# A hybrid HGRN2 / mLSTM / mixture-of-experts block: VectorE takes GpSimd's elementwise work, a head's sums use two PSUM rings, and three output tiles are added by DMA

## The chip, the cores and the metric

The kernel runs on one core of a Trainium2 chip. A core has a matrix engine (TensorE; PE in the rows, PEld for its weight loads), VectorE (DVE), ScalarE (ACT), GpSimd (POOL) and a queue engine (SyncE, SP) that issues most DMAs. Each engine runs its own instructions strictly in order, and engines wait for each other through semaphores. The metric is device microseconds (us) of one execution, lower is better; the time of a kernel is the median of its runs.

## The reference

The block works on 1024 tokens (16 more "meta" tokens stand in front) of width 1024, in fp32. Cut to what matters:

```python
h = layer_norm(concat([meta, x]))
proj = h @ w_in                                   # one wide projection, split in twelve
f = lb + (1 - lb) * sigmoid(f_a)                  # forget gate, 8 heads of 128
o_a = hgrn2(q_a, 1 - f, i_a, log(f))              # linear recurrence, decay per key channel
y_a = head_norm(o_a) * silu(g_a)                  # g_a is the projection GA in the kernel
h_b = mlstm(conv(q_b), conv(k_b), v_b, gates)     # 4 heads
y_b = head_norm(h_b) * sigmoid(o_b)               # o_b is the projection OB
mix = (sigmoid(gate_a) * (y_a @ w_a) + sigmoid(gate_b) * (y_b @ w_b)) @ w_out
h = layer_norm(ALPHA * h + mix)                   # first layer norm (ln1)
ffn = routed_experts(h) + shared_expert(h)        # 64 experts, 8 for each token
out = layer_norm(ALPHA * h + ffn)                 # last layer norm (ln2): gain g, bias b
```

## The kernel before

Every matrix product is made of three products of fp32r parts: a weight tile is split by ScalarE into a high part `wh` (a rounding copy) and by a subtraction into a low part `wl = raw - wh`. `load_slab` brings one 1024x512 slab of a weight as four pieces of 128x1024 through `split_weights` (lines 185 to 198): DMA on SP, `wh` on ACT (line 195), `wl` on VectorE or, for the pieces named by `SLAB_POOL = (1, 3)`, on GpSimd (line 196). There are 28 such slabs. The shared expert's six pieces do the same with `SHARED_POOL`, which adds three, so GpSimd makes 59 of these 118 subtractions.

The work runs in this order. (1) Embedding: layer norm of token tiles, transposes, first projection; GpSimd adds the bias there, and this is not touched. (2) The GA projection; `gate_out` (line 412) computes `silu(pm) * row` from the PSUM tile `pm`: sigmoid on ACT, a copy of `pm` on ACT, two products on GpSimd (lines 423, 424). Beside it `mlstm_gates` (line 507) computes the mLSTM gates with a few small matmuls (lines 530, 531), a chain on ACT and VectorE, and transposes (line 559). (3) Twice: projections F and Q, then four heads of `hgrn_head`. A head builds its score matrix `st` in seven doubling levels `lv` (lines 711 to 757). At each level VectorE makes `qp` (line 725), GpSimd makes `ks` (line 727), PE multiplies both into a PSUM tile (line 739), VectorE copies the result under a mask into `st` (line 742), GpSimd updates the suffix product (line 756) and VectorE the prefix product (line 757). The next level needs both. At the end of a head (lines 786 to 799) the output is made in two halves: PE sums `st`·`v` and `q`·`sts` into a PSUM tile from `ps_o`, a ring of one buffer, ACT takes sums of squares, VectorE a reciprocal root in 13 small steps (lines 116 to 127), and then `g = po * root * g` (line 799) frees the tile. (4) The remaining projections (the OB one with `gate_out` too), convolution, four mLSTM heads, gates. (5) The two branch products, the output product, ln1 (`layer_norm`, line 157, whose addition is on GpSimd for tiles 5, 6, 7), routing, the shared expert. (6) The routed experts, whose order on PE, GpSimd and SP is written out by hand. GpSimd there issues gathers (line 1359) and scatters that add into DRAM (line 1438). (7) The last layer norm, whose order on VectorE, ACT and GpSimd follows the table `TAIL`.

Outside the stretches whose order is written out, a scheduler sets the order of each engine's instructions when the program is built, from its own costs of the instructions. So a changed instruction also moves its neighbours.

In the last layer norm the eight token tiles `zf` are loaded by eight DMAs in turn. In `TAIL`, ('A', i) takes tile i's statistics on ACT (three instructions, `ACT_STATS`), ('S', i) takes them on VectorE, a group such as (('C2','C3','S4'), (0,1,2,3)) centres tiles on VectorE and between them runs the root of four tiles, and ('F', i) finishes a tile:

```python
if i in ADD_DVE:    # 3, 5, 7
    nc.vector.scalar_tensor_tensor(zs[i], zs[i], factor[i], b_ln2, op0=OP.mult, op1=OP.add)
else:
    nc.scalar.activation(zs[i], zs[i], AF.Copy, scale=factor[i])
    nc.gpsimd.tensor_add(zs[i], zs[i], b_ln2)
nc.sync.dma_start(out[i * P:(i + 1) * P, :], zs[i])
```

Of the kernel before, what the change touches and what calls it, by code (L numbers as in the profile page):

```python
# [14 lines left out]
AF = mybir.ActivationFunctionType  # L15
OP = mybir.AluOpType
# [3 lines left out]
P = 128  # L20
D = 1024
KT = 8
# [14 lines left out]
OH = 1  # L37
ACT_STATS = (1, 3, 5, 7)
XT = 6
# [8 lines left out]
SPREAD = 4  # L48
TAIL = (('A',1),('A',3),('S',0),('S',2),(('C0','C1'),()),('A',5),(('C2','C3','S4'),(0,1,2,3)),('F',0),('F',1),('A',7),('F',2),('F',3),('S',6),(('C4','C5','C6','C7'),(4,5,6,7)),('F',5),('F',4),('F',7),('F',6))
ADD_DVE = (3,5,7)  # L50
MUL_POOL = ()
ADD_POOL = (5,6,7)
SHARED_POOL = (1, 3, 5)
LATER = 300
# [16 lines left out]
def block_kernel(tc, A, out):  # L71
# [130 lines left out]
    def load_slab(src, c0):  # L202

        pairs = split_weights([src[k * 256:(k + 1) * 256, c0:c0 + 512].rearrange("(k p) n -> p k n", p=P)
                               for k in range(KT // 2)], 3000, on_pool=SLAB_POOL)
        hs = [t[:, c:c + 512] for t, _ in pairs for c in (0, 512)]
        ls = [t[:, c:c + 512] for _, t in pairs for c in (0, 512)]
        return hs, ls
# [204 lines left out]
    def gate_out(dst, c0, src, silu):  # L413
# [3 lines left out]
        def emit(pm, t0, n):  # L417
            s = stage_tile()
            nc.scalar.activation(s, pm, AF.Sigmoid)
            if silu:  # L420
                x = stage_tile()
                nc.scalar.activation(x, pm, AF.Copy)
                nc.gpsimd.tensor_mul(s, s, x)
            nc.gpsimd.tensor_mul(s, s, row)
            nc.sync.dma_start(dst[t0 - NM:t0 - NM + n, c0:c0 + 512], s)
# [251 lines left out]
    def hgrn_head(h, kss, st, zero):  # L677
# [30 lines left out]
        for lv in range(7):  # L708
# [17 lines left out]
            ks = kss[lv % 2]  # L726
            (nc.vector if lv in KS_DVE else nc.gpsimd).tensor_mul(sp(ks)[0], sp(kx)[0], s0)
            sc = ps_sc()
# [26 lines left out]
            else:  # L755
                (nc.vector if lv in SUF_DVE else nc.gpsimd).tensor_mul(s0, s0, p1[:, :, B - 1:B].to_broadcast([P, N, B]))
            nc.vector.tensor_mul(p1, p1, p0[:, :, B - 1:B].to_broadcast([P, N, B]))
# [28 lines left out]
        for gg in range(2):  # L786
            po = ps_o().rearrange("p (c t) -> p c t", t=P)
            s4 = slice(4 * gg, 4 * gg + 4)
# [458 lines left out]
    def load_piece(q):  # L1247
# [14 lines left out]
        loaded[q] = raw  # L1262

    steps = routing(scratch)

# [466 lines left out]
    def finish(i):  # L1732
        if i in ADD_DVE:
            nc.vector.scalar_tensor_tensor(zs[i], zs[i], factor[i], b_ln2, op0=OP.mult, op1=OP.add)
        else:
            nc.scalar.activation(zs[i], zs[i], AF.Copy, scale=factor[i])  # L1736
            nc.gpsimd.tensor_add(zs[i], zs[i], b_ln2)  # L1737
        nc.sync.dma_start(out[i * P:(i + 1) * P, :], zs[i])
# [117 lines left out]
```

## Time and profile before

| | |
|---|---|
| median of 3 runs | 2494.8 us (2491.28 to 2496.71) |
| profiled execution, its own time | 2498.45 us |
| its span, first to last instruction | 2496.7 us |
| mean granted clock of TensorE | 0.973 of full speed |
| PE / VectorE / ScalarE / GpSimd busy | 94% / 63% / 44% / 31% |

The profile is of one execution. Its times are counted from the start of the span. A row of instructions gives the time they were busy, their mean duration, and how long the engine sat idle just before them and which instruction ended that idle time. The granted clock of TensorE has two levels, 2.4 GHz (1.00) and 1.2 GHz (0.50); a value between them for a stretch is the mix of both.

### The profile page before, as it was taken

The page shows a single profiled execution, that of the slowest core. Times are in us where ns is not written, and L with a number is a line of the kernel's source. Part 1 is how long each engine was busy: PE and PEld are TensorE (multiplying, and loading weights), DVE is VectorE, ACT ScalarE, POOL GpSimd, SP SyncE. Part 2 cuts the span into 40 slices and gives each one's busy share as a digit, 9 for nine tenths or more (in the row PEclk, how much of TensorE's full clock was granted, in tenths as well). Part 3 has the DMA queues.
Part 4 walks back from the last instruction along what each step waited for, and adds up shares of the span by engine and source line. Part 5 has one row for each costly group of instructions (what it writes and reads, how often), then busy time and mean ns, then how long its engine had stood idle before and what let it go on. Part 6 is the DMA issues. An engine that isn't in the chain of part 4 may idle for free. (4 is left out here: it accounts for less than half of the span.)

```text
span 2496.7 us, 35578 instructions
## 1 busy us (share of the span) xinstructions
PE 2344.4 (94%) x12754; PEld 1878.5 (75%) x12754; DVE 1575.8 (63%) x2967; ACT 1107.3 (44%) x1858; POOL 762.1 (31%) x454
## 2 busy tenths in 40 slices
PE   6999989999899999999999999999999999999991
PEld 4788877987787987778777777777777777777760
DVE  8342776147721556412468487788888887888884
ACT  3342122321222236422233231677777776777772
POOL 3442344234412100011121220233433434444432
PEclk8999998999999999999999999999999999999996
DMA  6233231423322245444545323899999999999984
GB/s 243 89 104 115 68 121 56 140 84 99 94 89 86 97 149 187 134 135 152 175 156 170 121 98 131 271 301 334 328 320 322 319 328 317 319 313 330 302 268 149
DMA packets 203058, 475.15 MB, mean 190 GB/s; under 512 B 18672, under 2 KB 67504, under 8 KB 202880
## 3 DMA queue, kind: packets, MB, share of 16 engines
q1 hardware_dynamic: 181040, 396.24, 45.7%
q0 software_dynamic: 21088, 73.94, 12.5%
q10 hardware_dynamic: 752, 2.69, 0.3%
q8 instruction: 101, 1.65, 0.3%
q14 instruction: 77, 0.63, 0.1%
HBM read 370.59 MB, written 102.20 MB: 189 GB/s over the span
## 5 line engine op out<-in xcount | busy, mean ns | idle before, releaser
L196 POOL TENSOR_TENSOR wl<-wraw,wh 128x1024 fp32r<-128x1024 f32 x59 | 166.1, 2820 | 659.1 <-ACT wh L195 617.3
L1438 POOL DMA_INDIRECT acc<-yo,idx x95 | 189.8, 1998 | 509.8 <-DMA acc<-yo,idx 104.9
L135 PE MATMUL mm<-hL,wh 128*128 128x512 f32 (+2 forms) x768 | 280.4, 365 | 0.0
L134 PE MATMUL mm<-hH,wh 128*128 128x512 f32 (+2 forms) x768 | 280.2, 365 | 0.0
L136 PE MATMUL mm<-hH,wl 128*128 128x512 f32 (+2 forms) x768 | 280.1, 365 | 0.0
L196 DVE TENSOR_TENSOR wl<-wraw,wh 128x1024 fp32r<-128x1024 f32 x59 | 101.9, 1727 | 279.9 <-ACT wh L195 275.4
L136 PE MATMUL mm<-wh,hL 128*128 128x512 f32 x512 | 209.4, 409 | 5.3 <-DVE hL L345 5.2
L135 PE MATMUL mm<-wl,hH 128*128 128x512 f32 x512 | 207.1, 404 | 3.0 <-DVE wl L283 3.0
L134 PE MATMUL mm<-wh,hH 128*128 128x512 f32 x512 | 209.2, 409 | 0.0
L134 PEld LDWEIGHTS mm<-hH,wh 128*128 128x128 f32 x768 | 146.2, 190 | 17.5 <-issue 1.3
L135 PEld LDWEIGHTS mm<-hL,wh 128*128 128x128 f32 x768 | 146.2, 190 | 16.3 <-issue 0.2
L136 PEld LDWEIGHTS mm<-hH,wl 128*128 128x128 f32 x768 | 146.4, 191 | 15.8 <-issue 0.2
L1359 POOL DMA_INDIRECT xg<-h,idx x95 | 140.2, 1476 | 53.9 <-issue 24.4
L1505 DVE TENSOR_TENSOR wl<-eraw,wh 128x1024 fp32r<-128x1024 f32 x112 | 134.9, 1216 | 15.8 <-ACT wh L1504 15.4
L195 ACT ACTIVATE wh<-wraw 128x1024 fp32r<-128x1024 f32 x118 | 122.3, 1056 | 49.6 <-PE mm L135 36.7
L1505 DVE TENSOR_TENSOR wl<-wraw,wh 128x1024 fp32r<-128x1024 f32 x96 | 115.8, 1216 | 27.3 <-ACT wh L1504 27.0
L134 PE MATMUL mm<-wh,xh 128*128 128x512 f32 (+3 forms) x296 | 124.2, 419 | 0.0
L1504 ACT ACTIVATE wh<-eraw 128x1024 fp32r<-128x1024 f32 x112 | 117.0, 1060 | 13.9 <-PE mm L136 9.3
L136 PEld LDWEIGHTS mm<-wh,hL 128*128 128x128 f32 x512 | 98.4, 192 | 29.4 <-DVE hL L345 8.3
L136 PE MATMUL mm<-wh,xl 128*128 128x512 f32 (+3 forms) x296 | 117.9, 398 | 0.0
L135 PE MATMUL mm<-wl,xh 128*128 128x512 f32 (+3 forms) x296 | 117.3, 396 | 0.0
L135 PEld LDWEIGHTS mm<-wl,hH 128*128 128x128 f32 x512 | 98.6, 193 | 24.4 <-DVE wl L283 3.5
(546 smaller groups left out, 5883.8 us busy)
## 6 DMA issues: line engine op xcount, KB each, us to landing
eraw<-in_wexp_dram SPq DMA_DIRECT2D x210, 512.0 KB, 8.2
wraw<-in_wexp_dram SPq DMA_DIRECT2D x168, 512.0 KB, 7.8
wraw<-in_w_in_dram SPq DMA_DIRECT2D x72, 512.0 KB, 4.5
sgT<-st SPq DMA_DIRECT2D x32, 256.0 KB, 3.1
sg<-sgT SPq DMA_DIRECT2D x32, 256.0 KB, 4.1
wraw<-in_w_branch_a_dram SPq DMA_DIRECT2D x16, 512.0 KB, 4.2
wraw<-in_w_branch_b_dram SPq DMA_DIRECT2D x16, 512.0 KB, 4.5
wraw<-in_w_out_dram SPq DMA_DIRECT2D x16, 512.0 KB, 4.3
```

What stands on the lines that cost most here:

```text
L134: nc.tensor.matmul(o, ah, bh, start=start, stop=False)
L135: nc.tensor.matmul(o, ah, bl, start=False, stop=False)
L136: nc.tensor.matmul(o, al, bh, start=False, stop=stop)
L195: nc.scalar.activation(h, raw, AF.Copy)
L196: (nc.gpsimd if j in on_pool else nc.vector).tensor_sub(l, raw, h.bitcast(F32))
L1359: nc.gpsimd.indirect_dma_start(out=self.x, out_offset=None, in_=h1[:, :], in_offset=bass.IndirectOffsetOnAxis(ap=self.idx, axis=0))
L1438: self.out = nc.gpsimd.indirect_dma_start(out=acc[:, :], out_offset=bass.IndirectOffsetOnAxis(ap=self.idx, axis=0), in_=self.y, in_offset= ...
L1504: nc.scalar.activation(h, raw, AF.Copy)
L1505: (nc.gpsimd if j in POOL_SPLITS else nc.vector).tensor_sub(l, raw, h.bitcast(F32))
```

## The change

All elementwise work of GpSimd outside the embedding goes to VectorE: the `wl` subtractions of the 28 slabs and of the shared expert, both products of `gate_out` (the first now reads `pm` in PSUM, so the copy on ACT goes), `ks` and the suffix product in the heads, and the three additions of ln1. Only the copy and the fill of a head's level 0 (lines 719, 720) stay. The second half of a head's sums uses `ps_tr`, a ring of two buffers, in place of `ps_o`. In the last layer norm tile 4 moves its statistics to ACT, tile 6 takes tile 4's place on VectorE, tiles 3 to 7 are finished on VectorE, and for tiles 0, 1, 2 the bias is written to `out` long before by three DMAs, ACT scales the tile, and a DMA of GpSimd adds it to `out`.

```diff
-ACT_STATS = (1, 3, 5, 7)
+ACT_STATS = (1, 3, 4, 5, 7)
...
-TAIL = (('A',1),('A',3),('S',0),('S',2),(('C0','C1'),()),('A',5),(('C2','C3','S4'),(0,1,2,3)),('F',0),('F',1),('A',7),('F',2),('F',3),('S',6),(('C4','C5','C6','C7'),(4,5,6,7)),('F',5),('F',4),('F',7),('F',6))
-ADD_DVE = (3,5,7)
+TAIL = (('A', 1), ('A', 3), ('A', 5), ('A', 4), ('A', 7), ('S', 0), ('S', 2), (('C0', 'C1'), ()), (('C2', 'C3', 'S6'), (0, 1, 2, 3)),
+        ('F', 0), ('F', 1), ('F', 2), ('F', 3), (('C6', 'C5', 'C4'), ()), (('C7',), (4, 5, 6, 7)), ('F', 6), ('F', 5), ('F', 4), ('F', 7))
+ADD_DVE = (3, 4, 5, 6, 7)
 MUL_POOL = ()
-ADD_POOL = (5,6,7)
-SHARED_POOL = (1, 3, 5)
+ADD_POOL = ()
+SHARED_POOL = ()
...
-                               for k in range(KT // 2)], 3000, on_pool=SLAB_POOL)
+                               for k in range(KT // 2)], 3000)
...
             if silu:
-                x = stage_tile()
-                nc.scalar.activation(x, pm, AF.Copy)
-                nc.gpsimd.tensor_mul(s, s, x)
-            nc.gpsimd.tensor_mul(s, s, row)
+                nc.vector.tensor_mul(s, s, pm)
+            nc.vector.tensor_mul(s, s, row)
...
-            (nc.vector if lv in KS_DVE else nc.gpsimd).tensor_mul(sp(ks)[0], sp(kx)[0], s0)
+            nc.vector.tensor_mul(sp(ks)[0], sp(kx)[0], s0)
...
-                (nc.vector if lv in SUF_DVE else nc.gpsimd).tensor_mul(s0, s0, p1[:, :, B - 1:B].to_broadcast([P, N, B]))
+                nc.vector.tensor_mul(s0, s0, p1[:, :, B - 1:B].to_broadcast([P, N, B]))
...
-            po = ps_o().rearrange("p (c t) -> p c t", t=P)
+            po = ps_tr() if gg else ps_o().rearrange("p (c t) -> p c t", t=P)
...
+    for i in range(NT):
+        if i not in ADD_DVE:
+            nc.sync.dma_start(out[i * P:(i + 1) * P, :],
+                              bass.AP(tensor=A["ln2_b"].tensor, offset=A["ln2_b"].offset, ap=[[0, P], [1, D]]))
...
             nc.scalar.activation(zs[i], zs[i], AF.Copy, scale=factor[i])
-            nc.gpsimd.tensor_add(zs[i], zs[i], b_ln2)
+            nc.gpsimd.dma_start(out[i * P:(i + 1) * P, :], zs[i], accum_op=OP.add)
+            return
         nc.sync.dma_start(out[i * P:(i + 1) * P, :], zs[i])
```

The scheduler places the three new DMAs early, on SP right after the DMA of `nrow` at the end of the embedding. Three places of the new order matter. Line numbers of the changed kernel differ by one or two from those of the kernel before.

On TensorE, after the embedding, the small matmuls of `mlstm_gates` come in three groups of tokens (`gw` is their weight). Before, 22 of their 24 pairs of products stand together, and the last two pairs, of the third group, come 122 projection products later, between products of the GA projection:

```order
L530 MATMUL mm<-hH,gw 128x346
L136 MATMUL mm<-wh,hL 128x512
L531 MATMUL mm<-hL,gw 128x346
L134 MATMUL mm<-wh,hH 128x512
L530 MATMUL mm<-hH,gw 128x346
L135 MATMUL mm<-wl,hH 128x512
L531 MATMUL mm<-hL,gw 128x346
```

Now they too stand ahead of the GA projection:

```order
L529 MATMUL mm<-hH,gw 128x346
L530 MATMUL mm<-hL,gw 128x346
L135 MATMUL mm<-wh,hH 128x512
L136 MATMUL mm<-wl,hH 128x512
L137 MATMUL mm<-wh,hL 128x512
```

From the group's last matmul to the first transpose of the gates (line 559) there were 73 projection products, and there are 147 now.

On TensorE, at the end of a head, the sums of the first half stood before 22 projection products, and then those of the second half (again into `po`):

```order
L792 MATMUL po<-a_1994,a_1837 128x128
L791 MATMUL po<-v,st_945 128x128
L792 MATMUL po<-a_1994,a_1837 128x128
L136 MATMUL mm<-wh,hL 128x512
L134 MATMUL mm<-wh,hH 128x512
```

Now the second half follows at once, into `tr`, and the projection products come behind it:

```order
L791 MATMUL po<-a_1978,a_1821 128x128
L790 MATMUL po<-v,st_945 128x128
L791 MATMUL po<-a_1978,a_1821 128x128
L790 MATMUL tr<-v,st_945 128x128
L791 MATMUL tr<-a_1978,a_1821 128x128
```

On VectorE, in the levels of the second head, `qp`, the masked copy and the prefix product (`a_2083`) alternated:

```order
L757 TENSOR_TENSOR a_2083<-a_2083 128x128x4
L742 COPY_PREDICATED st_945<-lmask,sc 128x256x2
L725 TENSOR_TENSOR qp<-a_2084,a_2083 128x512
L742 COPY_PREDICATED st_945<-lmask,sc 128x128x4
L757 TENSOR_TENSOR a_2083<-a_2083 128x64x8
```

Now `ks` (`kss`) and the suffix product (`a_2083` is now the suffix, `a_2067` the prefix) stand among them, five instructions for a level:

```order
L755 TENSOR_TENSOR a_2083<-a_2083,a_2067 128x128x4
L756 TENSOR_TENSOR a_2067<-a_2067 128x128x4
L741 COPY_PREDICATED st_945<-lmask,sc 128x128x4
L724 TENSOR_TENSOR qp<-a_2068,a_2067 128x512
L726 TENSOR_TENSOR kss_944<-a_2077,a_2083 128x64x8
L755 TENSOR_TENSOR a_2083<-a_2083,a_2067 128x64x8
```

On TensorE 8, 10, 10, 10 and 8 projection products now stand between the level products of this head (46 in all), where there were 0, 3, 7, 2 and 11 (23).

## Rows read from the trace of the kernel before

**Rows 1.** The page's first part: busy time, share and instructions of each engine.

```profile
PE 2344.4 (94%) x12754; PEld 1878.5 (75%) x12754; DVE 1575.8 (63%) x2967; ACT 1107.3 (44%) x1858; POOL 762.1 (31%) x454
```

**Rows 2.** Stretches: length; PE, PEld, DVE, ACT, POOL busy; clock; DMA share; GB/s.

```profile
62.00:2440.00 2378.00, 2302.38 (x12593) 1846.55 (x12592) 1495.23 (x2770) 1070.44 (x1805) 726.12 (x433) 0.98 0.59 190
2440.00:2497.00 57.00, 2.54 (x11) 1.51 (x10) 30.02 (x57) 16.86 (x27) 16.89 (x7) 0.57 0.47 161
```

**Rows 3.** Timeline of the last layer norm: start, us, engine, line, operation, out<-in.

```profile
2456.51 1.06 ACT L1693 ACTIVATE dump<-zf 128x1024 f32<-128x1024 f32 x1 [13.34 <-DMA zf<-acc]
...
2459.20 1.06 ACT L1693 ACTIVATE dump<-zf 128x1024 f32<-128x1024 f32 x1
...
2467.66 1.28 DVE L1734 SCALAR_TENSOR_TENSOR zf<-zf,fr,wraw 128x1024 f32<-128x1024 f32 x1
...
2472.50 3.12 DVE L1728 SCALAR_TENSOR_TENSOR zf<-zf,fsm,wraw 128x1024 f32<-128x1024 f32 x1
...
2481.99 4.65 DVE L1734 SCALAR_TENSOR_TENSOR zf<-zf,fr,wraw 128x1024 f32<-128x1024 f32 x2
2483.21 5.62 POOL L1737 TENSOR_TENSOR zf<-zf,wraw 128x1024 f32<-128x1024 f32 x2 [5.41 <-ACT zf L1736]
```

**Rows 4.** The chain that ended last, its adding DMA: start, us, what.

```profile
2445.52 5.27 DMA acc<-yo,idx
```

**Rows 5.** What TensorE waited for: us in total, times, longest.

```profile
PE po L791 <- DVE g L799: 12.3, 4, 4.9
PE sc L739 <- DVE qp L725: 6.9, 9, 0.9
PE sc L739 <- POOL a L756: 6.3, 6, 1.9
...
PE tr L559 <- DVE igr L546: 3.7, 1, 3.7
...
PE tr L564 <- DVE diag L552: 1.9, 1, 1.9
```

**Rows 6.** Stretches that hold the first and the last four heads; columns as rows 2.

```profile
240.00:420.00 180.00, 161.92 (x1066) 136.20 (x1066) 132.51 (x287) 36.79 (x105) 76.56 (x51) 0.94 0.29 87
529.00:697.00 168.00, 152.74 (x1052) 127.64 (x1051) 128.26 (x285) 33.38 (x99) 71.95 (x46) 0.99 0.30 93
```

**Rows 7.** Three shorter stretches in which the clock fell; columns as rows 2.

```profile
140.00:160.00 20.00, 14.41 (x78) 13.43 (x77) 18.77 (x16) 9.33 (x16) 18.63 (x8) 0.83 0.45 139
360.00:420.00 60.00, 49.08 (x286) 42.18 (x285) 41.30 (x92) 9.35 (x30) 24.39 (x18) 0.83 0.22 65
1460.00:1482.00 22.00, 19.42 (x87) 16.24 (x86) 20.83 (x42) 8.71 (x10) 10.40 (x4) 0.84 0.12 48
```

**Rows 8.** Timeline of GpSimd, then of VectorE, in ln1.

```profile
1465.88 4.76 POOL L196 TENSOR_TENSOR wl<-wraw,wh 128x1024 fp32r<-128x1024 f32 x2
...
1468.33 2.33 DVE L127 SCALAR_TENSOR_TENSOR ln_sc<-rs_t,ln_sc 128x1 f32<-128x1 f32 x1
...
1471.09 0.16 DVE L127 SCALAR_TENSOR_TENSOR ln_sc<-rs_t,ln_sc 128x1 f32<-128x1 f32 x1
```

**Rows 9.** Timeline of a level of the second head; columns as rows 3.

```profile
293.56 1.81 POOL L727 TENSOR_TENSOR kss<-a,a 128x512 f32<-128x512 f32 x1
...
294.80 0.72 DVE L742 COPY_PREDICATED st<-lmask,sc 128x512 f32<-128x512 uint8 x1 [0.59 <-PE sc L739]
295.41 0.68 DVE L725 TENSOR_TENSOR qp<-a,a 128x512 f32<-128x512 f32 x1
295.45 1.61 POOL L756 TENSOR_TENSOR a<-a,a 128x512 f32<-128x512 f32 x1
...
296.28 1.93 PE L739 MATMUL sc<-qp,kss 128*128 128x64 f32 x16
```

**Rows 10.** Groups by line: busy us, mean ns; idle before (the first: 240 to 700).

```profile
L725 DVE TENSOR_TENSOR qp<-a,a 128x512 f32<-128x512 f32 x46 | 47.9, 1042 | 0.7
...
L196 POOL TENSOR_TENSOR wl<-wraw,wh 128x1024 fp32r<-128x1024 f32 x59 | 166.1, 2820 | 659.1 <-ACT wh L195 617.3 <-PE mm L136 39.5 <-DMA oB<-st 1.9
```

## The prediction

> **What bounds the kernel now.** The page's first part comes first: TensorE is busy 94% of the span, VectorE 63%, GpSimd 31% [rows 1]. A mean says nothing of single stages, so the stretches come next [rows 2]. From 62 to 2440 us TensorE works 2302 of 2378 us, at a granted clock of 0.98: 76 us of idle time is all that better order can win there, and 0.02 × 2378 = 48 us of clock. From 2440 on it does nothing; those 57 us are a chain of DMAs, ScalarE, VectorE and GpSimd, and each us cut out of it is a us of the span. The third view, what TensorE waited for, tells where the idle time sits near this change [rows 5]: 12.3 us for `g` of L799, which frees the only `po` tile; 13.2 us in the levels of a head, about half for VectorE and half for GpSimd; 5.6 us for the chain of the mLSTM gates. The last view is the clock by stretches [rows 6, 7]: it fell to half speed for a part of the head stretches, around 150 us, and in ln1, each time after such waits. So a gain must come from five places: the tail, the gates, the eight heads, ln1, and nowhere else. GpSimd's 59 subtractions are long (2.82 us each, [rows 10]), but no wait on a `wl` stands among the waits that I read; moving them away saves GpSimd time and not the kernel's.
>
> **The change part by part.** The sum is made on the profiled execution, 2498.45 us, which is 3.65 above the median of the runs shown (2494.8); the forecast is put on the median's basis at the end. A measurement of this kernel can tell about 0.2%, or 5 us, from no change.
>
> *The last layer norm: −7.5.* Before, it ends when GpSimd's two additions end, 2483.21 + 5.62 = 2488.83 [rows 3], and the output DMA follows, before and after alike. VectorE's rows beside GpSimd show a second price: one centring took 3.12 us and two finishes 4.65, against 1.28 for one that stood alone [rows 3]. After, VectorE reaches the finish of tiles 0 to 3 at 2467.66 as before. Then it has one finish (F3), four centrings, a root of 13 small steps (0.16 each where nothing disturbs, [rows 8]) and four finishes: 9 × 1.28 + 13 × 0.16 = 13.6, so 2481.3. ScalarE's statistics come every 2.69 us (2459.20 − 2456.51, [rows 3]); five of them from 2456.51 end at 2470.0, ahead of the second root. It then scales tiles 0 to 2 at about 1.06 each, by 2473.2, and the three adding DMAs start between 2471 and 2473. The nearest row of such a DMA is 5.27 us [rows 4]; one of 7 us would still land by 2480.4. So the end goes from 2488.8 to 2481.3. Bounds: 0, if the DMAs come one after another at 7 us or more (2471 + 21 = 2492), and −9.
>
> *The mLSTM gates: −9.* L559 and L564 wait 3.7 + 1.9 us for a chain on VectorE and ScalarE [rows 5], and in those 20 us the clock stands at 0.83, which costs 0.17 × 20 = 3.4 [rows 7]. The last two products of the gates now come early, and 147 instead of 73 projection products lie between them and the transposes. At 0.183 us for a mean TensorE instruction (2302/12593, [rows 2]) that is at least 13 us more cover for a wait of 5.6, so all 9.0 goes. Bounds −9 and −3, since part of the clock may fall for another reason.
>
> *The eight heads: −12, the most uncertain term.* Two things go. The second half's sums no longer wait for `g` of the first half: −12.3 [rows 5]. The clock in the two head stretches costs 0.06 × 180 + 0.01 × 168 = 12.5, of which 10.2 (0.17 × 60) lie between 360 and 420 [rows 6, 7]. The `po` waits are the longest in the heads, 4.9 against 1.9 for GpSimd's [rows 5]; I give them a little over two thirds of the 12.5, −8.9. Two things come. In a level GpSimd needed 1.81 + 1.61 us for `ks` and the suffix [rows 9]; on VectorE each costs what `qp` or the masked copy costs undisturbed, 0.68 to 0.72 [rows 9], but in the one queue that also holds those. After a level's `ks`, VectorE makes suffix and prefix (1.4 us), then the masked copy, which needs TensorE's 1.93 us of products [rows 9]; with 0.2 of latency a level takes 2.1 + 3 × 0.7 = 4.2 to 4.4 us. TensorE has 1.93 plus ten projection products at 0.183 or more, 3.8 to 4.0. It waits 0.4 at each of five levels of eight heads, 16 us, where 13.2 were lost: +3. And the second half's root, 13 × 0.16 = 2.1 us a head, now stands right behind the first half's, in front of the next head's levels; I charge a third of 8 × 2.1, +6. Sum −12.3 − 8.9 + 3 + 6 = −12. The best bound: all idle time (180 − 161.9 + 168 − 152.7 = 33.4) and the clock go, −46. The other: VectorE is busy 260.8 of the 348 us [rows 6]; GpSimd's 148.5 us there become about 60 at 0.69 in place of 1.71, so 321. Beside GpSimd `qp` took 1042 ns on average [rows 10] against 0.68 alone [rows 9]; 46 × 0.36 = 16.6 comes back, which leaves 304. TensorE's own work there is 314.6 − 12.5 = 302 at full speed. The two are now level, each must wait for the other in every level, and the worst bound is a loss, +60 (rival three).
>
> *ln1 and routing: −3.* The three additions and three shared pieces cost VectorE six operations of 1.28. In return GpSimd's long operations go, beside which a step of 0.16 us took 2.33 [rows 8]. The stretch 1460 to 1482 has 2.6 us of idle time and 0.16 × 22 = 3.5 of clock [rows 7]; half of both goes. Bounds −6 and +1.
>
> *Slab subtractions, `gate_out`: 0.* 59 × 1.28 = 76 us more on VectorE, which sits idle 37% of the time [rows 1]; TensorE's work on the slab before hides them. Without that cover a subtraction late by its 1.28 us would cost that much, at 28 slabs 36 us at the very most; below zero they can't go, since TensorE waited for none.
>
> *The three early DMAs: +1*, between 0 and +3. They move 0.5 MB each on SP's queue while the DMA engines are busy 59% [rows 2]; the next slab's loads stand behind them.
>
> Sum: −7.5 − 9 − 12 − 3 + 0 + 1 = −30.5: 2468 us on the profile's own time, 2464 on the median's.
>
> **The rivals.** *One: VectorE's queue takes GpSimd's place in the heads.* The 304 us of work and the 44 or more that a queue waiting in every level adds fill the 348; the waits at L791 turn into waits at the level products, and the clock falls as often. For it: the two loads are level. Against it: VectorE stood idle 87 us there, much of it behind GpSimd. The heads then give 0 and the kernel 2476. By the Trainium skill, "TensorE: Matmul & The Clock Gate", section "A second HAM failure mode: psum-queue depth-cycling", frequent short idles between groups of products alone make the clock alternate; the many level waits that stay would then keep the 12.5. The trace speaks rather against it: the second head stretch has level waits too, and a clock of 0.99 [rows 6].
>
> *Two: all of the heads' idle time and clock goes.* −46 in place of −12: 2430. Against it: the levels are a chain, 4.2 to 4.4 us long whatever TensorE does.
>
> *Three, slower: VectorE becomes the bound in the heads.* If no contention comes back and its 87 us of waiting stay, 321 + 87 = 408 us in place of 348, +60; with half of this, +30, the kernel is at 2506. It decides once VectorE's busy and idle time in the two stretches passes 348 + 18.5 = 366 us, the other terms' gain. The Trainium skill speaks for it in "Perfetto Trace Analysis", section "Optimizing Scalar/DVE Operations": work goes from a saturated VectorE to other engines, not onto it. The same place says that the two engines share a read port, so that sharing out may not help; the 1042 ns of `qp` agree with that [rows 10].
>
> *Four: the adding DMAs land last.* The tail gives nothing: 2472.
>
> **How the numbers follow.** Forecast 0.42; rival one 0.24, two 0.13, three 0.12, four 0.09. Predicted is the forecast's 2464. The range leaves out the ends of rivals two and three: 2436 to 2492. Its lower end is the forecast with most of rival two, its upper end the forecast's other terms with a loss of 16 in the heads. The forecast's own range is 2454 to 2472. Faster by over 0.2%: all but rival three and a tenth of the rest, 0.80; within 0.2% 0.08; slower 0.12.
>
> **What would show it.** Right: no wait of the sums for `g`; none of L559 and L564 (their numbers shift by one), and a clock of 1.00 around 150 us; the mean of `qp` near 0.7 us; the small root steps near 0.16 in ln1; the chain that ended last ends with a VectorE finish and its output DMA, some 7 us earlier after the last scatter. The two head stretches together shorter by 12 us, with VectorE above 85% busy in them. Wrong: waits of the level products for VectorE well over 16 us in sum, or the chain ending with an adding DMA; then the head term, or the tail term, has failed. Waits on `wl` would make the zero for the slabs wrong.

## The result and the profile after

The changed kernel takes 2415.45 us (2413.29 to 2419.14 in 5 runs) beside 2494.8 us for the kernel before (2491.28 to 2499.74): a ratio of 0.9682, 95% interval 0.9668 to 0.9696, or 79 us less. The prediction said 2464, range 2436 to 2492. The sign was right; the gain was more than twice what was forecast, and the time lies below the range.

First part of the page of the changed kernel:

```profile
PE 2315.7 (96%) x12754; PEld 1856.7 (77%) x12754; DVE 1592.9 (66%) x3148; ACT 1100.1 (46%) x1844; POOL 388.4 (16%) x270
```

VectorE got 181 more instructions and is busy only 17 us longer than in [rows 1]. The move alone should have brought 76 us for the subtractions and some 60 for the heads. So its other rows became some 120 us shorter; its own 59 subtractions account for 30 of that (1727 to 1221 ns each, below).

TensorE's span of 2411.5 us is 85.2 shorter (2496.7 before). 28.7 of it is TensorE's own busy time (2344.4 to 2315.7), which goes with the clock, since the products are the same; its mean granted clock rose from 0.973 to 0.987. The other 56.5 us is idle time. The two profiled executions lie 3.65 us above and 2.2 us below their medians, so 85.2 us in the traces stands for 79 in the medians. The two stretches of [rows 2], now:

```profile
62.00:2360.00 2298.00, 2273.69 (x12583) 1824.66 (x12582) 1517.65 (x2950) 1062.41 (x1787) 363.90 (x250) 1.00 0.60 196
2360.00:2411.00 51.00, 3.39 (x16) 2.08 (x15) 24.88 (x57) 17.69 (x32) 5.52 (x5) 0.58 0.62 180
```

Of the 76 us of idle time between embedding and tail, 24 are left, and the clock there is 1.00. To see where it went, both traces are cut at the same instructions on TensorE (the last transpose of the embedding, the first score product of the heads, their last sum into `po`, the first transpose of the branch products, the first product of the router, the first and the last product with `aux` in the experts). With the second ring, the last head's sums into `tr` follow 1.8 us behind that last sum into `po`; TensorE's counts, 2672 and 2674, show that the cut at `po` divides the work alike. The changed kernel, columns as rows 2:

```profile
82.20:238.10 155.90, 154.82 (x766) 130.95 (x765) 51.53 (x77) 55.92 (x83) 14.58 (x14) 1.00 0.30 99
238.10:653.50 415.40, 411.97 (x2674) 352.82 (x2673) 287.93 (x683) 99.54 (x245) 8.98 (x14) 1.00 0.34 105
653.50:999.50 346.00, 344.93 (x1711) 289.94 (x1710) 158.86 (x321) 131.41 (x274) 0.13 (x2) 1.00 0.38 127
999.50:1255.80 256.30, 253.77 (x1142) 204.66 (x1142) 109.44 (x189) 72.36 (x93) 0.95 (x1) 1.00 0.49 168
1255.80:1468.90 213.10, 204.43 (x1065) 167.59 (x1064) 158.75 (x503) 59.58 (x95) 2.71 (x2) 1.00 0.40 137
1468.90:2259.10 790.20, 783.84 (x4647) 592.02 (x4647) 657.91 (x1011) 564.17 (x872) 297.72 (x192) 0.99 0.97 312
2259.10:2411.50 152.40, 103.66 (x510) 73.14 (x506) 104.43 (x188) 89.07 (x146) 37.15 (x28) 0.86 0.79 237
```

The kernel before, the heads and the three stages behind them:

```profile
242.40:697.50 455.10, 421.77 (x2672) 359.45 (x2670) 281.11 (x602) 103.13 (x260) 179.10 (x114) 0.97 0.31 96
697.50:1053.80 356.30, 349.49 (x1711) 292.88 (x1709) 149.94 (x278) 130.55 (x267) 49.47 (x26) 0.99 0.37 125
1053.80:1318.90 265.10, 257.65 (x1144) 207.41 (x1144) 103.93 (x171) 72.38 (x93) 49.40 (x19) 0.99 0.49 161
1318.90:1547.60 228.70, 213.88 (x1062) 174.09 (x1062) 164.71 (x488) 59.50 (x95) 39.78 (x17) 0.96 0.38 128
```

All stages beside each other, in us:

| stage | length before, after | difference | TensorE idle before, after | clock before, after |
|---|---|---|---|---|
| embedding | 83.2, 82.2 | −1.0 | 23.1, 23.9 | 0.92, 0.94 |
| GA projection, gates | 159.2, 155.9 | −3.3 | 6.1, 1.1 | 0.98, 1.00 |
| first to last head | 455.1, 415.4 | −39.7 | 33.3, 3.4 | 0.97, 1.00 |
| projections, convolution, mLSTM | 356.3, 346.0 | −10.3 | 6.8, 1.1 | 0.99, 1.00 |
| branch products | 265.1, 256.3 | −8.8 | 7.5, 2.5 | 0.99, 1.00 |
| output product, ln1, routing | 228.7, 213.1 | −15.6 | 14.8, 8.7 | 0.96, 1.00 |
| experts | 790.5, 790.2 | −0.3 | 6.0, 6.4 | 0.99, 0.99 |
| last experts and last layer norm | 158.6, 152.4 | −6.2 | | |

So 39.7 us are in the heads, 34.7 in the three stages behind them, for which little was forecast, and 6.2 at the end.

The gates' stage needs care. In the execution shown its clock is 1.00, but in the traces of eight of the runs below, which have the same early products of the gates, the clock falls to 0.50 for 10 to 17 us from about 135 us on, though TensorE waits for nothing there. It falls while TensorE alternates single transposes of the gates with single products (in the execution shown from 130.8 to 140.7 us), 0.58 us a pair where a product alone takes 0.23. The run with idle fills shows the clock (columns as rows 2):

```profile
140.00:150.00 10.00, 10.00 (x25) 6.42 (x25) 2.29 (x9) 2.56 (x4) 3.28 (x5) 0.52 0.20 57
```

In seven of them, cut at the same instructions, the stage takes 160 to 163 us, no less than the 159.2 of before. So its 3.3 us are those of one execution.

What TensorE still waits for in the changed kernel, a selection down to the levels (total, times, longest):

```profile
PE sc L137 <- DVE al L1419: 3.8, 10, 0.9
...
PE po L1492 <- DVE oh L1477: 3.1, 1, 3.1
...
PE tr L1105 <- DVE yl L1074: 2.6, 1, 2.6
...
PE sc L704 <- DVE a L699: 1.4, 3, 0.8
...
PE sc L738 <- DVE qp L724: 0.2, 1, 0.2
```

No wait of the sums for `g`, none of the gates' transposes, and 0.2 us in the levels, against 12.3, 5.6 and 13.2 in [rows 5].

One level of a head now, on VectorE (start, us, line):

```profile
291.40 0.71 DVE L741 COPY_PREDICATED st<-lmask,sc 128x512 f32<-128x512 uint8 x1 [0.76 <-PE sc L738]
292.01 0.68 DVE L724 TENSOR_TENSOR qp<-a,a 128x512 f32<-128x512 f32 x1
292.61 0.68 DVE L726 TENSOR_TENSOR kss<-a,a 128x512 f32<-128x512 f32 x1
293.33 0.69 DVE L755 TENSOR_TENSOR a<-a,a 128x512 f32<-128x512 f32 x1
294.06 0.69 DVE L756 TENSOR_TENSOR a<-a 128x512 f32<-128x512 f32 x1
295.53 0.72 DVE L741 COPY_PREDICATED st<-lmask,sc 128x512 f32<-128x512 uint8 x1 [0.79 <-PE sc L738]
```

A level is 4.13 us long (295.53 − 291.40), and in it VectorE waits 0.8 us for TensorE, not the other way round. TensorE's ten projection products of this level, from 291.18 to 293.60, take 2.4 us, and the level's own products 1.90. The groups of [rows 10] read now (the first from 236 to 655 us, the second over the whole program):

```profile
L724 DVE TENSOR_TENSOR qp<-a,a 128x512 f32<-128x512 f32 x46 | 31.6, 688 | 0.0
...
L197 DVE TENSOR_TENSOR wl<-wraw,wh 128x1024 fp32r<-128x1024 f32 x118 | 141.5, 1221 | 216.5 <-ACT wh L196 212.5
```

`qp` fell from 1042 to 688 ns. All 118 subtractions together take VectorE 141.5 us. Before, its 59 alone took 101.9, and GpSimd's 59 the 166.1 of [rows 10]:

```profile
L196 DVE TENSOR_TENSOR wl<-wraw,wh 128x1024 fp32r<-128x1024 f32 x59 | 101.9, 1727 | 279.9 <-ACT wh L195 275.4 <-PE mm L136 4.4
```

The last layer norm (the rows that answer to [rows 3]):

```profile
2377.80 1.06 ACT L1697 ACTIVATE dump<-zf 128x1024 f32<-128x1024 f32 x1 [13.75 <-DMA zf<-acc]
...
2388.91 1.28 DVE L1738 SCALAR_TENSOR_TENSOR zf<-zf,fr,wraw 128x1024 f32<-128x1024 f32 x1
...
2391.31 3.67 DVE L1732 SCALAR_TENSOR_TENSOR zf<-zf,fsm,wraw 128x1024 f32<-128x1024 f32 x3
...
2393.01 1.91 POOL L1741 DMA_DIRECT2D out_dram<-zf  x2 [24.74 <-DMA out_dram<-zf]
...
2397.46 4.87 DVE L1738 SCALAR_TENSOR_TENSOR zf<-zf,fr,wraw 128x1024 f32<-128x1024 f32 x4
```

From ScalarE's first statistics to the last finish it is 2402.33 − 2377.80 = 24.5 us, where it was 2488.83 − 2456.51 = 32.3: 7.8 less. Three centrings in a row take 3.67, four finishes 4.87, no row is lengthened, and the adding DMAs start 9 us before the end.

### The profile page after: what moved, and what is told of

Same layout as the page of the kernel before. It is cut to its first block, busy times and chain, and to the rows that moved or that the text cites. A ratio compares the mean times of both kernels' runs of the same rounds, so it can differ in the third digit from the quotient of the medians.

```text
span 2411.5 us, 35454 instructions
## 1 busy us (share of the span) xinstructions
PE 2315.7 (96%) x12754; PEld 1856.7 (77%) x12754; DVE 1592.9 (66%) x3148; ACT 1100.1 (46%) x1844; POOL 388.4 (16%) x270
## 5 line engine op out<-in xcount | busy, mean ns | idle before, releaser
L197 DVE TENSOR_TENSOR wl<-wraw,wh 128x1024 fp32r<-128x1024 f32 x118 | 141.5, 1221 | 216.5 <-ACT wh L196 212.5
L1442 POOL DMA_INDIRECT acc<-yo,idx x95 | 183.7, 1934 | 517.1 <-ACT xh L173 112.6
L137 PEld LDWEIGHTS mm<-hH,wl 128*128 128x128 f32 x768 | 144.7, 188 | 15.6 <-issue 0.2
L196 ACT ACTIVATE wh<-wraw 128x1024 fp32r<-128x1024 f32 x118 | 122.7, 1056 | 55.0 <-PE mm L136 37.4
L1509 DVE TENSOR_TENSOR wl<-wraw,wh 128x1024 fp32r<-128x1024 f32 x96 | 115.8, 1216 | 27.3 <-ACT wh L1508 26.6
L1508 ACT ACTIVATE wh<-eraw 128x1024 fp32r<-128x1024 f32 x112 | 117.0, 1060 | 13.2 <-PE mm L137 8.8
L135 PEld LDWEIGHTS mm<-wh,hH 128*128 128x128 f32 x512 | 97.7, 191 | 21.6 <-PE mm L530 0.9
```

The costliest lines, as they stand in the source:

```text
L135: nc.tensor.matmul(o, ah, bh, start=start, stop=False)
L137: nc.tensor.matmul(o, al, bh, start=False, stop=stop)
L196: nc.scalar.activation(h, raw, AF.Copy)
L197: (nc.gpsimd if j in on_pool else nc.vector).tensor_sub(l, raw, h.bitcast(F32))
L1442: self.out = nc.gpsimd.indirect_dma_start(out=acc[:, :], out_offset=bass.IndirectOffsetOnAxis(ap=self.idx, axis=0), in_=self.y, in_offset= ...
L1508: nc.scalar.activation(h, raw, AF.Copy)
```

## The experiments

Theory A: GpSimd's operations hinder VectorE's rows beside them, and TensorE waits for the chains that become late. Theory B: something else paid, the single po tile in the heads, a late `wl` or the new order elsewhere. Times are medians beside runs of the kernel before on the same chip, which took 2494.95 to 2496.35; how much slower a run is than the changed kernel is the difference from 2415.45. The program has 13055 rows on TensorE.

### One edit at a time, on the kernel before

**The second po ring alone.**

```diff
-            po = ps_o().rearrange("p (c t) -> p c t", t=P)
+            po = ps_tr() if gg else ps_o().rearrange("p (c t) -> p c t", t=P)
```

> The kernel before with one edit: the second half of a head's sums uses ps_tr. After the change the heads (first score product to last sum on TensorE) are 39.7 us shorter, far more than the 12 that was forecast. Theory A (VectorE and GpSimd hinder each other, and GpSimd's ks and suffix set the length of a level): the ring alone removes the 12.3 us of waits at L791 and some clock, 10 to 20 us, and the level waits stay or grow. Theory B (the single po tile was what held the heads): the ring alone gives 30 to 40 us.

2496.3 us beside 2496.2, ratio 0.9997 (0.9985 to 1.0009): nothing. Neither theory had that. The waits at L791 are gone, but others stand in their place:

```profile
PE sc L705 <- DVE rs_t L123: 12.2, 6, 2.3
PE sc L739 <- DVE qp L725: 12.1, 10, 4.0
...
PE sc L705 <- DVE a L700: 10.8, 6, 2.6
```

TensorE now waits for the root steps, for `qp` and for the first product of the next head. The wait for `g` was where the lateness of VectorE and GpSimd showed, not what made it.

**`ks` and the suffix product alone.**

```diff
-KS_DVE = (6,)
-SUF_DVE = (5,)
+KS_DVE = tuple(range(7))
+SUF_DVE = tuple(range(7))
```

> The kernel before with ks and the suffix product of every level on VectorE, one po tile. Theory A: the level waits (13.2 us) and the clock loss tied to them go, qp falls from 1042 ns to about 700; 10 to 25 us faster. Theory B: the waits at L791 for the only po tile stay or grow, since VectorE has more in front of g; 0 to 8 us, or slower.

2480.0 us, ratio 0.9930 (0.9914 to 0.9947): 16 us, as theory A said. `qp` fell to 783 ns, not to 700. That the subtractions still ran on GpSimd doesn't explain it alone: with them there, `qp` is at 722 in the run with both edits of the heads and at 690 in the changed kernel with the subtractions put back.

**The subtractions alone.**

```diff
-                               for k in range(KT // 2)], 3000, on_pool=SLAB_POOL)
+                               for k in range(KT // 2)], 3000)
-SHARED_POOL = (1, 3, 5)
+SHARED_POOL = ()
```

> The kernel before with the wl subtractions of the slabs and of the shared expert on VectorE. After the change the stretch between the heads and the experts is 34.7 us shorter, where 3 was forecast. Theory A (GpSimd's 2.8 us subtractions lengthen VectorE's rows beside them, and TensorE waits for those): 15 to 35 us faster, L196 on VectorE falls from 1727 to about 1220 ns. Theory B (that stretch was freed by something else, the three additions of ln1, gate_out, or the order that came out): within 5 us of before.

2451.8 us, ratio 0.9826 (0.9808 to 0.9844): 44 us, more than half of the whole gain, from the part that was costed at nothing, and more than theory A's upper end of 35. In its trace (an execution 6.5 us below its median) the heads are 17 us shorter, though not a line of them was changed, the three stages behind them 28, the gates' stage 4:

```profile
235.80:673.80 438.00, 415.55 (x2677) 352.41 (x2676) 276.38 (x613) 102.76 (x260) 148.16 (x102) 1.00 0.32 99
```

L196 fell to 1263 ns. The waits of L559 and L564 went here too. The scheduler also made a new order on TensorE: the gates' last products come at 94 us, not at 126. This run alone doesn't part the two.

**Both edits of the heads.** Ring, `KS_DVE` and `SUF_DVE` as above.

> The kernel before with both edits of the heads, the second po ring and ks and suffix on VectorE; the subtractions stay on GpSimd. If the two add up, this is the sum of the two single runs; if each needs the other (the ring so that g does not hold TensorE, VectorE so that a level is short), it is more than their sum. Theory A: 30 to 45 us faster, all of the heads' gain. Theory B: no better than the ring alone.

2472.4 us, ratio 0.9905 (0.9889 to 0.9922): 24 us, 8 more than the sum of the two (16 + 0), but less than theory A expected (30 to 45). So beside the other edit the ring is worth something; the rest of the heads' gain must come with the subtractions or the order that came with them.

**The last layer norm alone**, with its three early DMAs; TensorE's order is that of before.

> The kernel before with the new last layer norm alone (and its three early DMAs); TensorE's order is that of before. The forecast for the tail was -7.5 and for the early DMAs +1, and the changed kernel's tail was 7.8 us shorter from the first statistics on ScalarE to the end. Expected 5 to 9 us faster than before. Rival: the tail only became shorter because the DMA queues stood better in the changed kernel; then within 3 us.

2486.0 us, ratio 0.9961 (0.9947 to 0.9976): 10 us (6 to 13), as expected or a little more.

### One edit taken back, on the changed kernel

**Subtractions back.** The reverse of the diff above.

> The changed kernel with the wl subtractions of pieces 1 and 3 (of the shared expert 1, 3 and 5) back on GpSimd. Theory A: the same loss as with the idle subtractions, 25 to 45 us, less some that VectorE no longer works. Theory B with a late wl: the same loss here, but none with the idle subtractions. If the gains of the change simply add up, this is 2415 + 44 = 2459.

2449.8 us, ratio 0.9824 (0.9806 to 0.9842), 34 us slower than the changed kernel.

**`ks` and suffix back.**

```diff
-            nc.vector.tensor_mul(sp(ks)[0], sp(kx)[0], s0)
+            (nc.vector if lv in KS_DVE else nc.gpsimd).tensor_mul(sp(ks)[0], sp(kx)[0], s0)
```

and the same for the suffix product.

> The changed kernel with ks and the suffix product back on GpSimd in the levels where they were before. In the kernel before this edit alone gave 16 us, with the ring 24. Theory A: 15 to 25 us slower than the changed kernel, qp back above 850 ns. A rival: the level waits came from the subtractions beside them, then within 6 us.

2448.9 us, ratio 0.9813 (0.9797 to 0.9830), 33 us slower: twice what the same edit gave on the kernel before, and above theory A's 25. `qp` is at 840 ns, and TensorE waits for the root, as in the run with the ring alone:

```profile
PE sc L704 <- DVE rs_t L124: 13.6, 6, 2.3
...
PE sc L704 <- DVE a L699: 9.2, 6, 1.9
```

**One po ring.** The reverse of the ring's diff.

> The changed kernel with one po tile (ps_o for both halves). The ring alone gave the kernel before nothing (2496.3 against 2496.2), and 8 us beside the edits of the heads (2480.0 to 2472.4). Theory A: 5 to 15 us slower than the changed kernel, the waits for g come back. A rival: VectorE is now fast enough to free po in time, then within 4 us.

2416.5 us, ratio 0.9682 (0.9660 to 0.9705), the changed kernel's own. The expectation of theory A was wrong, the rival's right: with GpSimd silent, VectorE frees `po` in time (the waits for `g` are 0.5 us in all).

### Idle work on GpSimd

The edits above also move the order. These runs keep it and only add work whose result nobody reads.

**An idle subtraction** for each one that was moved, over the spent raw tile:

```diff
-                res.append((h, l))
+                res.append((h, l)); j % 2 and nc.gpsimd.tensor_sub(raw, raw, h.bitcast(F32))
```

> The changed kernel, and for the pieces whose wl GpSimd made before, GpSimd now makes the same subtraction once more over the spent raw tile, whose result nobody reads (only the next load into that tile waits for it). The order on TensorE and on VectorE stays that of the changed kernel but for 4 and 6 rows. Moving the subtractions alone gave 44 us (2496.2 to 2451.8). Theory A (hindrance: GpSimd's long subtractions lengthen the VectorE rows beside them, and chains on which TensorE waits become late): 25 to 45 us slower than the changed kernel, 2440 to 2460, and the lengthened rows are back. Theory B (a wl that came late, or the new order that the scheduler made, was what paid): within 6 us of the changed kernel, 2415 to 2421.

2462.9 us (2455.8 to 2471.6), ratio 0.9860 (0.9841 to 0.9879): 47 us slower, with TensorE's order the same but for 4 rows of 13055. Four groups by line, VectorE's subtraction, GpSimd's idle one, and two of the branch stage on VectorE (busy us, mean ns); below them the changed kernel's `ml`:

```profile
L197 DVE TENSOR_TENSOR wl<-wraw,wh 128x1024 fp32r<-128x1024 f32 x118 | 195.8, 1683 | 209.3 <-ACT wh L196 204.7 <-PE mm L137 3.7
...
L198 POOL TENSOR_TENSOR wraw<-wraw,wh 128x1024 f32<-128x1024 f32 x59 | 162.5, 2754 | 893.6 <-DVE wl L197 834.6 <-issue 35.6 <-DVE top L1126 22.2
...
L1000 DVE TENSOR_TENSOR yl<-tr,yh 128x512 fp32r<-128x512 f32 x32 | 21.0, 682 | 27.4 <-ACT yh L999 27.4
...
L1026 DVE TENSOR_TENSOR ml<-part,mh 128x512 fp32r<-128x512 f32 x16 | 16.6, 1039 | 8.5 <-ACT mh L1025 8.5
```

```profile
L1026 DVE TENSOR_TENSOR ml<-part,mh 128x512 fp32r<-128x512 f32 x16 | 11.1, 691 | 8.4 <-ACT mh L1025 8.4
```

`wl` went from 1221 to 1683 ns, `ml` (two operands in SBUF) from 691 to 1039; `yl`, whose operand `tr` is in PSUM, stayed at 682. Four rows of each group started while an idle subtraction ran: all four of `ml` were held, and none of `yl`. In this trace (an execution 8.7 us above its median) the heads are 17 us longer than in the changed kernel and the three stages behind them 35. This shows hindrance: no `wl` comes from GpSimd here, and the order is the same.

**The same on the kernel with only the subtractions moved.**

> The kernel before with the subtractions on VectorE (2451.8), and GpSimd makes them once more over the spent raw tile. TensorE's order is that of the run without the idle work but for 52 of 13055 rows. If all of the 44 us were hindrance, this is 2490 to 2500 again, or more, since VectorE now carries the work too; if a part was the new order or a wl that came late, that part stays won, and this is 2455 to 2485.

2490.7 us, ratio 0.9986 (0.9972 to 1.0000). 39 of the 44 us come back. By stages, of the 28 us that the three stages behind the heads had gained, all come back (854.5 us, 850.1 before); the heads (445.3) stay 10 us shorter than before and the gates' stage (155.3) 4. So the stages behind the heads were hindrance. For the gates the order is what stays; in the heads it may be the order or a `wl` that came late, which the runs don't part.

**An idle fill** in place of the subtraction (`nc.gpsimd.memset(raw, 0.0)`).

> The changed kernel, and for pieces 1 and 3 (of the shared expert 1, 3 and 5) GpSimd fills the spent raw tile with zeros, where the run before it made an idle subtraction there (47 us slower than the changed kernel). Orders on TensorE and VectorE are those of that run. A fill only writes. If any GpSimd access to on-chip memory hinders VectorE, the loss goes with GpSimd's busy time: a fill of 128x512 took 0.56 us in the changed kernel, so 1.1 against 2.8 us, 15 to 20 us slower than the changed kernel. If it is the subtraction's reading that hinders, within 5 us.

2421.2 us, ratio 0.9694 (0.9665 to 0.9723): no difference from the changed kernel that can be told. The fills were busy 57.4 us in all, against 162.5; at the subtractions' price for a us of busy time they would have cost 17 us (47 × 57.4 / 162.5), and the interval ends 10 us above the changed kernel.

**Two idle copies** (`nc.gpsimd.tensor_copy(raw, h)`, twice), one operand read and one written.

> The changed kernel, with two idle copies by GpSimd of wh over the spent raw tile in place of the one idle subtraction (which cost 47 us; one fill cost about 5 and was busy 0.97 us against 2.75). Two copies should keep GpSimd busy for about 2 x 1.3 us, near to the subtraction's 2.75. If the busy time of GpSimd is what hinders, 30 to 47 us slower than the changed kernel; if it is the subtraction's two operands read at once, a copy with one operand hinders little, 0 to 12 us.

2442.7 us, ratio 0.9797 (0.9781 to 0.9814): 27 us slower, between the two expectations. GpSimd was busy as long as with the subtractions:

```profile
L198 POOL COPY wraw<-wh 128x1024 f32<-128x1024 f32 x118 | 168.9, 1438 | 865.3 <-DVE wl L197 859.8 <-DVE left L1129 1.8
```

So busy time alone does not set the price: 169 us of copies cost 27, 163 us of subtractions 47. A copy reads one operand and not two, but it is also half as long (1438 against 2754 ns); no run parts these.

**Idle products in the heads**, into a tile nobody reads; VectorE's and TensorE's orders are exactly those of the changed kernel (the two additions, cut out of their lines):

```diff
+            lv < 6 and nc.gpsimd.tensor_mul(idle.rearrange("p (m b) -> p m b", b=B), sp(kx)[0], sp(kx)[0])
...
+                lv < 5 and nc.gpsimd.tensor_mul(idle.rearrange("p (m b) -> p m b", b=B), sp(kx)[0], sp(kx)[0])
```

> The changed kernel, and in the levels of a head GpSimd makes a product of the same shape beside each ks and suffix product that it made before (five and four a head), of data that stays as it is, into a tile that nobody reads. TensorE's and VectorE's orders are exactly those of the changed kernel. With ks and suffix back on GpSimd the kernel took 33 us more (2448.9). Theory A (hindrance, as with the idle subtractions): 20 to 33 us slower than the changed kernel, qp back above 850 ns. Rival (the length of GpSimd's own two products in a level's chain was the price): within 6 us, and the 33 us are the chain's.

2458.6 us, ratio 0.9850 (0.9831 to 0.9868), 43 us slower, more than theory A's upper end; `qp` stayed at 687 ns, which theory A had wrong. The products read only `k`, so they all ran at once when `k` was there, beside the second half's root. This stretch of the timeline shows the mechanism row by row (VectorE and GpSimd, in order of start):

```profile
325.15 0.69 DVE L726 TENSOR_TENSOR kss<-a,a 128x512 f32<-128x512 f32 x1
325.20 1.55 POOL L726 TENSOR_TENSOR idle<-a 128x512 f32<-128x512 f32 x1 [1.29 <-DVE rs_t L124]
325.76 1.00 DVE L126 TENSOR_TENSOR rs_t<-rs_t,rs_v 128x4 f32<-128x4 f32 x1
...
326.77 0.68 DVE L699 TENSOR_TENSOR a<-a,a 128x512 f32<-128x512 f32 x1
326.82 1.53 POOL L755 TENSOR_TENSOR idle<-a 128x512 f32<-128x512 f32 x1
327.37 0.99 DVE L128 SCALAR_TENSOR_TENSOR ss<-rs_t,ss 128x4 f32<-128x4 f32 x1
...
328.30 0.68 DVE L720 TENSOR_TENSOR a<-a 128x512 f32<-128x512 f32 x1
...
328.43 1.45 POOL L726 TENSOR_TENSOR idle<-a 128x512 f32<-128x512 f32 x1
328.90 1.00 DVE L124 TENSOR_TENSOR rs_t<-ss 128x4 f32<-128x4 f32 x1
...
334.15 2.90 PE L704 MATMUL sc<-a,a 128*128 128x192 f32 x8 [3.81 <-DVE st L706]
```

The two take turns. Each product of GpSimd runs to its end while the VectorE row that started behind it is held: a step on 128x4 numbers that takes 0.16 us alone takes 1.00, and ends with GpSimd's product. GpSimd is held too (1.55 us, where 1.04 was its shortest in this stretch). The second half's root, from its first product to its last step, lasts from 324.97 to 335.89 us here, 10.9 us; in the changed kernel the same rows, with the same neighbours between them, take 4.6. The masked copies behind them are late, and TensorE waits for `st`:

```profile
PE sc L704 <- DVE st L706: 23.1, 7, 3.9
```

The heads are 455.5 us long here, beside 417.2 in the changed kernel (both to the very last sum); the stages behind them are as long as there, 814.4 and 813.6.

**The same products inside the levels**, where `ks` and suffix had been: they read `sp(ks)[0]` instead of `sp(kx)[0]`.

> The changed kernel with GpSimd's idle products in the heads again, but each now reads the ks of its level, so that they start inside the levels, where GpSimd made ks and suffix before; in the run before them they ran in one bunch ahead of the levels, beside the root, and cost 43 us. TensorE's and VectorE's orders are exactly those of the changed kernel. Theory A1 (an idle product costs wherever VectorE has work to do): again 20 to 43 us. Theory A2 (it costs where VectorE's small steps stand in a chain on which TensorE waits, as in the root; in a level VectorE has 0.8 us of idle time that takes it up): 0 to 12 us, and the 33 us of putting ks and suffix back come from what GpSimd does ahead of the levels and from its own chain.

2435.1 us, ratio 0.9752 (0.9735 to 0.9768): 20 us slower, the lower end of A1, above A2. The heads are 432.4 us long. TensorE's waits in the levels are 5.2 us (0.2 in the changed kernel), and those at the first product of the next head 9.4 (1.4). So a product costs less here than beside the small steps of a root, but it costs. It also leaves 13 of the 33 us of putting `ks` and suffix back unexplained; they may be GpSimd's own chain, the rival, which no run shows alone.

### Further in the same direction

**The embedding's additions and first subtractions too** (`SLAB_POOL = ()`, `HX_DVE = tuple(range(-1, 8))`), and **its subtractions alone** (`SLAB_POOL = ()`).

> The changed kernel and the same move in the embedding: the first slabs' subtractions and the additions of the bias to VectorE, which is busy 50.4 of the first 62 us there. Theory A carried on (hindrance costs more than VectorE's added work): 2 to 8 us faster than the changed kernel. Rival (there VectorE is the bound, and has no idle time to take the work): 3 to 15 us slower.

> As the run before, but only the first slabs' subtractions go to VectorE; GpSimd keeps the additions of the bias. Between the changed kernel and that run: theory A 1 to 5 us faster, the rival 0 to 6 us slower.

2420.0 us, ratio 0.9699 (0.9682 to 0.9716), and 2420.9 us, ratio 0.9694 (0.9675 to 0.9712). Both intervals overlap the changed kernel's: not faster. In the embedding VectorE is already busy 50.4 of 62 us; the work that it takes over and the hindrance that goes seem to balance, which these runs don't show apart. No version beat the changed kernel.

## Why the prediction was off

**The step that failed: "Slab subtractions, `gate_out`: 0".** It asked who waits for the moved result, found that nobody waits for a `wl`, and costed the move at nothing, even saying that below zero it can't go. Measured, the subtractions alone were worth 44 us, idle ones took 39 of these back, and idle ones on the changed kernel cost 47. What they delayed was not `wl` but the rows of VectorE that started behind them with operands in SBUF alone. The rows for this were read: 2.33 us for a step of 0.16 beside a subtraction [rows 8], centrings of 3.12 against 1.28 [rows 3], `qp` at 1042 ns [rows 10]. But they were used only in the tail, in ln1 and as a credit of VectorE's busy time in the heads, never for TensorE's waits in the heads, the branch products and routing. Three stages behind the heads got −3 in the sum and gave −34.7; in the run with the subtractions alone they gave 28. The prediction let a gain come from five places "and nowhere else", but TensorE stood idle 29.1 us in these stages before (6.8 + 7.5 + 14.8 in the table), and 12.3 are left.

**The heads: −12 forecast, −39.7 measured; mis-sized, from two errors.** The first: 12.3 + 8.9 were booked to the ring. The ring gave 0 on the kernel before, 8 beside the other edit, and 1 when taken out of the changed kernel; there the waits for `g` vanish with one tile too, through VectorE's speed. The second: the charges of +3 for longer levels and +6 for the root did not come. The length of a level was right (4.2 to 4.4 worked out, 4.13 measured), but TensorE had enough of its own: the ten products in between take 2.4 us, where 0.183 each made 1.8, and with 1.9 of the level's own they fill it. TensorE waits 0.2 us in all levels together, and VectorE's 0.8 per level are its own slack. VectorE's load was put at 304 us for 348 us of stretch; over two stretches of that length (222 to 402 and 487 to 655 us) it is 269 (137.99 + 130.87), 77% and not the 85% that was to show a right forecast, since more than the 16.6 us of `qp` came back. Hence the best bound nearly came out, idle time from 33 to 3 us and a clock of 1.00. Rival two, at 0.13, was nearly what happened, and its objection, that a level is a chain, does not matter as long as TensorE has other work in it.

**The gates: −9 forecast, −3.3 measured; the mechanism right, the size not.** The waits are gone through the cover, as forecast: with 144 to 147 products in between TensorE waits for no transpose, also with the idle subtractions beside them, and with 57, in the changed kernel with the subtractions back, it waits 4.6 us. But the early order came with the subtractions, since the run that moved only them has it. What failed is the size of what the waits and the clock were to bring: in their place TensorE alternates transposes and products for 10 us, busy but slow, and in eight runs the clock falls there, after which the stage is no shorter than before.

**Right in size:** the tail (−7.5; 7.8 in the trace, 10 alone). The early DMAs cost nothing that shows. The experts stayed as they were.

**Rivals one, three and four fell.** VectorE did not become the bound: it was busy only 17 us longer. The clock rule of rival one (the page of the Trainium skill that it names) could not be tried, since the idles went; with the idle subtractions the mean clock fell again (0.975 to 0.980 in four runs, 0.983 to 0.987 in five of the changed kernel) as waits came back.

**What adds up.** Singly, on the kernel before: 44 (subtractions) + 24 (both edits of the heads) + 10 (tail) = 78 of 79. Taken back singly, 34 + 33 + 1. That the first sum comes out is in part luck, since the parts are not independent: the ring gave 0, 8 or 1, `ks` and suffix 16 or 33. `gate_out` and the additions of ln1 were not tried alone, and their worth is open: by the first sum 1 us is left for them, but the changed kernel with the subtractions back is 46 us faster than the kernel before (2496.2 to 2449.8), where ring, heads and tail account for 34.

## What to carry to other kernels

Before costing work on GpSimd as free because it sits off the critical path, compare each VectorE group's mean with its shortest row of the same form: a mean well above it, or a tiny step that takes a microsecond, was here the sign that GpSimd held it up. The price of such an operation was the waits behind VectorE, most of all where a chain of small steps was waited for, and it can be measured by adding an idle copy of the operation that nobody reads. A wait that a trace names (here for `g`) may only be the place where lateness shows; taking it away alone moved it elsewhere. And a clock read from one execution may be luck: here another execution with the same order stood at the low level for up to 17 us.

## What the runs showed of the hardware

VectorE's rows with two operands in SBUF are held by a GpSimd operation that reads, for as long as that lasts: 0.16 us became 1.00. Rows with an operand in PSUM were not (`yl`, 682 and 683 ns with and without). A row with one operand can be held too: in the kernel before this step of the last layer norm ended with GpSimd's additions, at 2477.8 us, and the step L795 was held all eight times that it started beside a running operation of GpSimd (up to 1.84 us, 0.17 at its shortest).

```profile
2475.53 2.30 DVE L1709 TENSOR_SCALAR fr<-fr 128x4 int32<-128x4 int32 x1
```

Fills (write only, 0.97 us each) made no difference that can be told, copies cost 27 us, subtractions 47, at about the same busy time for the last two. The Trainium skill states this in "SBUF — State Buffer", section "Who interferes with whom": a VectorE instruction with two SBUF inputs contends with a GpSimd instruction that reads SBUF, not with one that only writes; the shared ports are "an exclusive lock", and "Issue order, not op shape, decides who blocks." The traces agree, with the numbers above (0.16 to 1.00 us for the row that started later); that copies cost less than subtractions of the same busy time no run here explains.

TensorE's clock goes with 28.7 of the 85.2 us, though its products are the same; in the execution shown it stood at 1.00 from the gates to the routing once the waits were gone. Waits are not its only cause: in eight runs with the gates' products early it fell to 0.50 for 10 to 17 us from about 135 us on, where TensorE waited for nothing but alternated transposes and products.
